# Stores of a FiLM layer: small DMAs for the first rows, whole slabs for the rest

## The chip, the core and the metric

One core of one Trainium2 chip. The metric is the device time of one execution in microseconds; the profile's span (first to last instruction) is about 1.8 us shorter.

## The reference

```python
# x [32, 512, 256], conditioning [32, 64], gamma_proj and beta_proj [64, 256], all float32
gamma = conditioning @ gamma_proj
beta = conditioning @ beta_proj
return x * (1 + gamma[:, None, :]) + beta[:, None, :]
```

16.78 MB are read, 16.78 MB are written, and each element has one multiplication and one addition.

## The kernel before

x lies in SBUF as four slabs of 128 partitions x 32 rows x 256 floats: 32 KB per partition, contiguous in HBM. All four fit at once, so no buffer is reused. Loads are issued by SyncE, the small loads and the stores by ScalarE. Of each group of 16 rows VectorE takes 11 and GpSimd 5; the group is then stored.

```python
LOADS = {0: [8, 24]}          # slab 0 in two loads, the others whole
GROUP = 16
ON_DVE = 11
# ...
nc.scalar.dma_start(out=cond_s, in_=conditioning)
# ... gbproj[:, :dim] <- gamma_proj, gbproj[:, dim:] <- beta_proj, also from nc.scalar
for s in range(SLABS):
    xs = xpool.tile([P, ROWS, dim], f32, name=f"xs{s}")
    # ... nc.sync.dma_start of LOADS.get(s, [ROWS]) rows each
# ... two small matmuls give gamma and beta per slab, in PSUM (gb_p) and in SBUF (gb_s)
for s in range(SLABS):
    # ...
    for r0 in range(0, ROWS, GROUP):
        # ... v = rows r0 to r0+10, w = rows r0+11 to r0+15
        nc.vector.scalar_tensor_tensor(out=v, in0=rows(g_p, nv), scalar=1.0, in1=v,
                                       op0=ALU.add, op1=ALU.mult)
        nc.gpsimd.tensor_tensor(out=w, in0=w, in1=rows(g_s, nw), op=ALU.mult)
        nc.vector.tensor_add(out=v, in0=v, in1=rows(b_p, nv))
        nc.gpsimd.tensor_tensor(out=w, in0=w, in1=rows(b_s, nw), op=ALU.add)
        nc.scalar.dma_start(out=o_v[s, :, r0 : r0 + GROUP, :],
                            in_=xs[:, r0 : r0 + GROUP, :])
```

## Time and profile before

| | before |
|---|---|
| first three runs | 84.46, 86.00, 86.02 us |
| span of the profiled (fast) run | 82.6 us |
| bytes moved, mean rate over the span | 33.69 MB, 408 GB/s |
| VectorE / GpSimd busy | 60% / 56% |
| last addition on VectorE ends | 66.6 us |
| last store packet ends | 81.38 us |

The rows of the page that carry the argument are shown in the prediction: slices, queues, chain, stretches and issues. Two habits help in reading them. The chain of waits ends with the last instruction of a compute engine; where stores follow, look at what the DMA row does after that. And a DMA packet (one contiguous run of bytes that one of the 16 DMA engines moves, here 1 to 32 KB of data) is booked in the slice in which it starts; here most packets last up to 1.2 us, so the GB/s of one slice can be off by a fifth or more in either direction. Where the text speaks of packet records, packets were counted by queue and size in the same trace. A load or store lands when its completion semaphore, the counter that tells the program of it, has its last count; in the first profile of each kernel that is 0.3 to 1.6 us after its last data packet ends.

### The profile page before, as it was taken

Reading aid. Unit: us, or ns where it says so; the run is one execution under the profiler, and the core shown is the slowest. Engines: PE = TensorE matmul, PEld = TensorE weight load, DVE = VectorE, ACT = ScalarE, POOL = GpSimd, SP = SyncE. Lnnn points to the kernel's source line nnn. Section 1 sums busy time; section 2 is a strip of 40 time slices with the busy share of each in tenths; the row PEclk is TensorE's granted clock in tenths of the full one; section 3 lists DMA queues with packets and bytes.
Section 4 is the critical chain, followed back from the end, with each engine's and each line's share of the span. In section 5 each row is a group of like instructions: output and inputs, shape, how many; then the busy total and the mean of one; then the engine's idle time right before and its main releaser. Section 6 shows DMA issues by size and latency. Waiting matters only on the chain.

```text
span 82.6 us, 156 instructions
## 1 busy us (share of the span) xinstructions
PE 9.1 (11%) x10; PEld 2.8 (3%) x10; DVE 49.9 (60%) x18; ACT 3.9 (5%) x9; POOL 46.2 (56%) x22
## 2 busy tenths in 40 slices
PE   0080000899600000000000000000000000000000
PEld 0100000443000000000000000000000000000000
DVE  2011000059999999999999999999999920000000
ACT  0600000034400000000000000000000000000000
POOL 2000000069999999999999999999995000000000
DMA  3899999969969989998889979899999999999992
GB/s 56 337 508 397 389 397 524 460 302 508 508 270 492 508 381 381 413 476 381 381 381 556 460 302 460 381 468 421 429 452 389 468 421 421 460 389 452 437 421 87
DMA packets 2080, 33.69 MB, mean 408 GB/s; under 512 B 288, under 2 KB 416, under 8 KB 416
## 3 DMA queue, kind: packets, MB, share of 16 engines
q1 hardware_dynamic: 720, 16.78, 48.6%
q10 hardware_dynamic: 1360, 16.92, 48.0%
HBM read 16.92 MB, written 16.78 MB: 408 GB/s over the span
## 4 chain that ended last, share of the span: by engine, by line
DVE 49%; DMA 16%; issue 11%; PE 2%; ACTq 1%; ACT 1%
DVE xs L100 30%; DVE xs L103 19%; DMA gbproj<-in_beta_proj_dram 16%; PE gb_p L79 2%; ACTq L50 1%; ACTq L48 0%; ACT gb_s L82 0%; ACT gb_s L85 0%
## 5 line engine op out<-in xcount | busy, mean ns | idle before, releaser
L102 POOL TENSOR_TENSOR xs<-xs,gb_s 128x1280 f32<-128x1280 f32 x8 | 23.0, 2895 | 16.2 <-ACT gb_s L82 16.2
L100 DVE SCALAR_TENSOR_TENSOR xs<-gb_p,xs 128x2816 f32<-128x2816 f32 x8 | 24.7, 3083 | 10.9 <-ACT gb_s L85 10.9
L103 DVE TENSOR_TENSOR xs<-xs,gb_p 128x2816 f32<-128x2816 f32 x8 | 24.7, 3086 | 0.3
L104 POOL TENSOR_TENSOR xs<-xs,gb_s 128x1280 f32<-128x1280 f32 x8 | 23.0, 2893 | 0.0
L79 PE MATMUL gb_p<-gbproj,cond_T 64*128 64x512 f32 x8 | 7.2, 1074 | 8.9 <-DMA gbproj<-in_beta_proj_dram 8.9
L74 DVE COPY cond_T<-cond_T_p 64x512 f32<-64x512 f32 x1 | 0.7, 683 | 4.3 <-PE cond_T_p L72 4.3
L79 PEld LDWEIGHTS gb_p<-gbproj,cond_T 64*128 64x128 f32 x8 | 2.5, 328 | 13.7 <-issue 13.7
L72 PE MATMUL cond_T_p<-rident,cond_s 32*64 32x512 f32 x2 | 1.9, 1065 | 3.9 <-DMA cond_s<-in_conditioning_dram 3.9
L82 ACT ACTIVATE gb_s<-gb_p 128x256 f32<-128x256 f32 x4 | 1.5, 383 | 16.4 <-PE gb_p L79 16.4
L85 ACT COPY gb_s<-gb_p 128x256 f32<-128x256 f32 x4 | 1.5, 367 | 0.0
L82 ACT ACT_TABLE_LOAD x1 | 1.3, 1283 | 2.4 <-issue 2.4
L67 DVE COPY rident<-ident 32x512 f32<-32x512 f32 x1 | 0.4, 416 | 1.2 <-POOL ident masks.py:199 1.2
L72 PEld LDWEIGHTS cond_T_p<-rident,cond_s 32*64 32x64 f32 x2 | 0.3, 202 | 3.9 <-issue 3.9
masks.py:197 POOL MEMSET ident<- 32x32 f32 x1 | 0.1, 114 | 0.3 <-POOLq L121 0.3
masks.py:199 POOL TENSOR_SCALAR_AFFINE_SELECT ident<-ident 32x32 f32<-32x32 f32 x1 | 0.2, 202 | 0.1
L121 POOL MEMSET const-float32-0.0<- 128x1 f32 x1 | 0.1, 103 | 0.2 <-issue 0.2
L121 POOL MEMSET const-bfloat16-1.0<- 128x1 bf16 x1 | 0.1, 106 | 0.0
L121 POOL MEMSET const-uint8-127<- 128x1 uint8 x1 | 0.1, 106 | 0.0
L121 POOL MEMSET const-float32-1.0<- 128x1 f32 x1 | 0.1, 103 | 0.0
## 6 DMA issues: line engine op xcount, KB each, us to landing
out_dram<-xs ACTq DMA_DIRECT2D x8, 2048.0 KB, 18.2
xs<-in_x_dram SPq DMA_DIRECT2D x3, 4096.0 KB, 32.9
xs<-in_x_dram SPq DMA_DIRECT2D x1, 3072.0 KB, 12.2
xs<-in_x_dram SPq DMA_DIRECT2D x1, 1024.0 KB, 4.6
gbproj<-in_gamma_proj_dram ACTq DMA_DIRECT2D x1, 64.0 KB, 9.1
gbproj<-in_beta_proj_dram ACTq DMA_DIRECT2D x1, 64.0 KB, 12.9
cond_s<-in_conditioning_dram ACTq DMA_DIRECT2D x1, 8.0 KB, 3.0
```

Of the source, the lines that this page charges most:

```text
L50: nc.scalar.dma_start(out=gbproj[:, :dim], in_=gamma_proj)
L67: nc.vector.tensor_copy(out=rident.rearrange("p (b g) -> p b g", g=REP), in_=ident.to_broadcast([batch, batch, REP]),)
L72: nc.tensor.matmul(cond_T_p, lhsT=cond_s, rhs=rident, start=True, stop=True)
L74: nc.vector.tensor_copy(out=cond_T, in_=cond_T_p)
L79: nc.tensor.matmul(p_t, lhsT=cond_T[:, s * P : (s + 1) * P], rhs=gbproj, start=True, stop=True)
L82: nc.scalar.activation(out=s_t[:, :dim], in_=p_t[:, :dim], func=mybir.ActivationFunctionType.Identity, bias=1.0, scale=1.0)
L85: nc.scalar.copy(out=s_t[:, dim:], in_=p_t[:, dim:])
L100: nc.vector.scalar_tensor_tensor(out=v, in0=rows(g_p, nv), scalar=1.0, in1=v, op0=ALU.add, op1=ALU.mult)
L102: nc.gpsimd.tensor_tensor(out=w, in0=w, in1=rows(g_s, nw), op=ALU.mult)
L103: nc.vector.tensor_add(out=v, in0=v, in1=rows(b_p, nv))
L104: nc.gpsimd.tensor_tensor(out=w, in0=w, in1=rows(b_s, nw), op=ALU.add)
L121: nc = _bacc.Bacc("TRN2", target_bir_lowering=False, num_devices=1)
```

## The change

The intent, as far as the code shows it: the first store shares the DMA engines with the loads, and small packets there let the loads pass; later stores go out in the longest runs possible, with less fixed cost per packet.

```diff
     LOADS = {0: [8, 24]}
+    STORES = {0: (2, 4, 8, 16, 32), 1: (32,), 2: (32,), 3: (32,)}
 ...
-            nc.scalar.dma_start(out=o_v[s, :, r0 : r0 + GROUP, :],
-                                in_=xs[:, r0 : r0 + GROUP, :])
+            done = r0 + GROUP
+            if done in STORES[s]:
+                e0 = 0
+                for e1 in STORES[s]:
+                    if r0 < e1 <= done or STORES[s] == (ROWS,):
+                        nc.scalar.dma_start(out=o_v[s, :, e0:e1, :], in_=xs[:, e0:e1, :])
+                    e0 = e1
```

The numbers in `STORES` are the rows at which a store ends.

## The prediction

> **What bounds the kernel now.** I read five views of the profile of the kernel before, in this order: the slices with the DMA queues, the chain of waits, the groups with their waits, a table of four stretches, and the list of instructions in order of time. Where they did not suffice I counted the trace's packet records by queue and size.
>
> The slices and the queues come first, because the kernel moves 33.69 MB and does little else:
>
> ```profile
> DMA  3899999969969989998889979899999999999992
> DMA packets 2080, 33.69 MB, mean 408 GB/s; under 512 B 288, under 2 KB 416, under 8 KB 416
> q1 hardware_dynamic: 720, 16.78, 48.6%
> q10 hardware_dynamic: 1360, 16.92, 48.0%
> ```
>
> The reader is to see that the 16 DMA engines are busy from the second slice to the last but one, and that the two queues together take 48.6 + 48.0 = 96.6% of the span of 82.6 us, or 79.8 us. The packet records say the same: the first data packet starts at 1.74 us and the last ends at 81.38, which is 79.64 us; from 4 us on, a count of the packets in flight never falls below about 16. No engine waits for work. (The dips to 6 or 7 in the slices are an effect of booking a packet where it starts; the packets of 32 KB take 1.21 us.) q1 is the loads of x, q10 the stores with the three small loads.
>
> The chain of waits tells another story, and has to be read with care:
>
> ```profile
> DVE 49%; DMA 16%; issue 11%; PE 2%; ACTq 1%; ACT 1%
> ...
> 57.37 3.09 DVE xs L103
> 60.46 3.01 DVE xs L100
> 63.47 0.02 issue
> 63.49 3.09 DVE xs L103
> ```
>
> It ends with the last addition on VectorE, at 66.58 us, 16 us before the span does, because the chain does not follow the stores. What happens in those 16 us is in the stretches (columns: busy time of the engines, clock, DMA share, GB/s) and in the issues:
>
> ```profile
> 2.00:12.50 10.50, 1.93 (x2) 0.29 (x2) 0.68 (x1) 1.28 (x1) 0.00 (x0) 1.00 0.97 400
> 12.50:27.50 15.00, 7.16 (x8) 2.50 (x8) 9.91 (x4) 2.59 (x8) 10.20 (x4) 1.00 1.07 456
> 27.50:50.00 22.50, 0.00 (x0) 0.00 (x0) 22.40 (x8) 0.00 (x0) 22.50 (x9) 1.00 0.97 408
> 50.00:81.00 31.00, 0.00 (x0) 0.00 (x0) 16.48 (x6) 0.00 (x0) 12.97 (x5) 1.00 1.01 431
> ```
> ```profile
> out_dram<-xs ACTq DMA_DIRECT2D x8, 2048.0 KB, 18.2
> xs<-in_x_dram SPq DMA_DIRECT2D x3, 4096.0 KB, 32.9
> ```
>
> Stores alone run at 431 GB/s to the end. A store of 2 MB would take 4.9 us at that rate, yet its median time from issue to landing is 18.2 us: stores stand in a queue. When the last is issued at 66.67 us, 6.27 MB of stores have still to start by the packet records, of which it is 2.10. So the end is set by bytes over DMA rate, and computing is hidden with a reserve of 4.17 MB / 431 GB/s = 9.7 us.
>
> **The skill.** The Trainium skill, "DMA: Bandwidth & Descriptors", section "Where 436 GB/s comes from", gives 435 GB/s as the ceiling of the 16 ports. The trace agrees: 431 with stores alone, and the packet records, spread evenly over their durations, give 433 with loads alone. The same page, "Queues, rings and completion order", says that each engine goes round-robin between the queues that have work, a packet at a time. The trace agrees: from 30 to 48 us one engine's sequence is mostly one load packet of 32 KB, one store packet of 16 KB, in turn. The same page, "Why small descriptors are slow (HBM only)", names a fixed cost per packet. The trace shows it, small: 16 KB take 611 ns and 32 KB 1213 ns, so 602 ns for 16 KB of data and 9 ns fixed; 8 KB (309 ns) and 1 KB (46 ns) fit the same line.
>
> **The change part by part.** The arithmetic on VectorE and GpSimd stays in the same order. Eight stores remain eight stores; only their sizes and moments change.
>
> 1. Packets. Before: 8 stores x 128 partitions = 1024 packets of 16 KB, 64 per engine, 64 x 611 ns = 39.1 us. After, per engine: 16 of 2 KB, 8 of 4 KB, 8 of 8 KB, 8 of 16 KB, 24 of 32 KB, again 64. By the line above, 16 x 84 ns (my estimate) + 8 x 160 (estimate) + 8 x 309 + 8 x 611 + 24 x 1213 = 1.34 + 1.28 + 2.47 + 4.89 + 29.11 = 39.09 us. The long packets save 24 x 9 ns = 0.2 us and the short ones give it back. Sum: zero.
>
> 2. The first rows leave earlier. In the built program the first three stores (rows 0 to 7) wait for VectorE alone, whose part of the group ends at 20.64 + 3.09 = 23.73 us; before, the store of 16 rows waited for GpSimd too and was issued at 25.94. So they are issued at about 23.8, 24.2 and 24.5. The first store took 29.76 - 25.94 = 3.8 us from issue to its first packet, behind load packets already taken up, so I expect the first store packet at about 27.6. On full engines this makes nothing faster; it shifts the order.
>
> 3. Loads get nearly all of the rate while they last. At 27.6 us each engine has 11 load packets of 32 KB to start (5.77 MB / 16 / 32 KB). With one store packet of 2 KB between two loads, they take 11 x 1.225 + 10 x 0.09 = 14.4 us from 28.2 (the packet in hand finishes first), so the last load ends near 42.6 us instead of 48.6. No computing waits for it, before or after: GpSimd takes up slab 3 at 51.5 us and VectorE at 54.25, and their views of waits show no wait for x. Worth zero.
>
> 4. Whole slabs wait for both groups. The first halves of slabs 1 to 3 are issued later by one group (about 4.8 us for slab 1: 42.17 instead of 37.35); the last issue stays at 66.67. The question is whether the stores run dry. From 42.6 us stores run alone with 16.45 MB left. By 54.4 (slab 2 issued) 5.1 MB more are done, 5.4 in all of 8.39 issued: 3.0 MB in hand, 6.9 us. By 66.67, 0.33 + 24.1 us x 431 = 10.7 MB are done of 12.58: 1.9 MB in hand, 4.4 us, against a start of a store of 3.8 us in the worst case seen (cond_s at the start needed 1.4 us from issue to first packet). The reserve shrinks from 9.7 us to 4.4 but is not used up. Cost zero, with the smallest margin of all steps.
>
> 5. Stretched packets. Before, load packets are stretched to 1.35-1.66 us at two moments, about 28.5 and 32.3 us, some 2.5 us after the first two stores were issued: roughly (12 x 0.3 + 8 x 0.22) / 16 = 0.3 us per engine. The change may lose some of this or repeat it. I credit -0.3 us.
>
> End of the wire: 42.6 + 16.45 MB / 431 GB/s (38.2) = 80.8 us, against 81.38. The sum of the parts is -0.3 to -0.6 us, the span 82.6 - 0.4 = 82.2.
>
> **Rivals.** (a) The stores run dry before slab 3 is issued. For it: the margin in 4 is 4.4 us, and it rests on the loads finishing at 42.6. Against: a store issued onto a busy queue need not pay the whole 3.8 us. It would show as a gap of up to 2 us near 70 us, and 86 to 87 us. (b) Loads now finish late because 32 KB store packets take a half share instead of a third, and VectorE waits for slab 3. For it: round-robin by packets. Against: by 42.17 us, when the first store of 32 KB runs is issued, the loads are nearly done, and 16 small packets with two rows of turns stand ahead. It would need the loads to end 9 us later than I work out. It would give 86 to 88 us. (c) Reads and writes mixed cost rate, and less mixing pays: the stretch from 27.5 to 50 us moves 408 GB/s against 431. If all of that were regained, 22.5 x (1 - 408 / 431) = 1.2 us, so 83.2 from the fast mode. Against: spread over their durations the packets of 35 to 50 us move 431 to 433, so most of the difference is booking.
>
> **Range and chances.** The three runs before are 84.46, 86.00 and 86.02 us, and the profiled one 84.35: two modes 1.6 us apart, unexplained by the one profile. The change should give 84.1 in the lower and 85.7 in the upper; not knowing which the median falls in, I say 85.0 us, 83.7 to 86.4. A gain over 2% needs rival (c) together with a fall into the lower mode: 0.08. A loss over 2% needs (a) or (b) in full: 0.05. Within 2%: 0.87.
>
> **What would show it.** Right: DMA slices of 9 to the end as before; the last load lands near 43 us and the small stores stay between 15 and 20 us in the queue; VectorE runs from 17.5 to 66.6 without a wait; the last stores run at 431 GB/s; the span is near 82.2. Step 4 is wrong if a slice near 70 us drops; step 3 if VectorE or GpSimd wait for x; step 1 if 2 KB packets take much more than 84 ns; step 5 if the mixed stretch is much slower or faster. The whole is wrong if the last packet ends before 79 or after 83 us.

## The result

The changed kernel takes 84.50 us (median of 6, 84.39 to 84.61); the kernel before, with three more runs beside it, 84.64 (six runs, two of them at 86.0). Executions over 1.5% slower than the fastest of the same kernel are left out of the means. Ratios here are the mean of one kernel's fast runs over the mean of the other's fast runs of the same rounds, so not quite the ratio of medians: 0.9993, with a 95% interval of 0.9977 to 1.0008. The time is the same. The forecast of 85.0 held as a range and as a class, but against the 86.0 then known it announced 1.0 us less, or 1.2%, and 0.07% came. That forecast of a gain was wrong.

Profile after, slices and queues:

```profile
DMA  3899999899699699996979999998996998999790
DMA packets 2080, 33.69 MB, mean 408 GB/s; under 512 B 288, under 2 KB 416, under 8 KB 800
q1 hardware_dynamic: 720, 16.78, 48.5%
q10 hardware_dynamic: 1360, 16.92, 47.9%
```

The number of packets is the same to the last one, 2080, although 384 more of them are now under 8 KB; the shares of the queues add up to 96.4% of 82.7 us, 79.7 us as before. The issues:

```profile
out_dram<-xs ACTq DMA_DIRECT2D x3, 4096.0 KB, 17.2
out_dram<-xs ACTq DMA_DIRECT2D x1, 2048.0 KB, 22.3
out_dram<-xs ACTq DMA_DIRECT2D x1, 1024.0 KB, 21.5
out_dram<-xs ACTq DMA_DIRECT2D x2, 256.0 KB, 16.9
out_dram<-xs ACTq DMA_DIRECT2D x1, 512.0 KB, 20.3
xs<-in_x_dram SPq DMA_DIRECT2D x3, 4096.0 KB, 23.0
```

A store of 256 KB, 0.6 us of transfer at 431 GB/s, takes 16.9 us to land: it goes one packet of 2 KB at a time between load packets of 32 KB. The loads of whole slabs land in 23.0 us (median) instead of 32.9. (Part of that is only a later issue: the build reuses semaphores differently, so slab 2's load is now issued at 10.73 us instead of 2.10 and slab 3's at 13.97 instead of 10.3. Slab 1's packets fill the queue until 22 us, so it costs nothing. The prediction had not seen it.) The end of the chain:

```profile
57.95 3.09 DVE xs L104
61.04 3.01 DVE xs L101
64.05 0.02 issue
64.07 3.09 DVE xs L104
```

The same last addition, 0.6 us later because gamma and beta landed 0.6 us later in this execution, without a wait in between: no row of the waits of VectorE or GpSimd names x. The stretches of the prediction, after:

```profile
2.00:12.50 10.50, 1.93 (x2) 0.28 (x2) 0.68 (x1) 1.28 (x1) 0.00 (x0) 1.00 1.00 400
12.50:27.50 15.00, 7.16 (x8) 2.50 (x8) 9.35 (x4) 2.59 (x8) 9.63 (x4) 1.00 0.99 422
27.50:50.00 22.50, 0.00 (x0) 0.00 (x0) 22.40 (x8) 0.00 (x0) 22.50 (x9) 1.00 1.01 431
50.00:81.00 31.00, 0.00 (x0) 0.00 (x0) 17.06 (x6) 0.00 (x0) 13.57 (x5) 1.00 1.00 431
```

Here lies a trap. From 27.5 to 50 us the changed kernel moves 431 GB/s against 408, just as rival (c) would have it, and yet ends no sooner: what it gains in the third row it lacks in the second (422 against 456). Cut the same two traces at 27, 44 and 50 us. Before:

```profile
27.00:44.00 17.00, 0.00 (x0) 0.00 (x0) 16.93 (x6) 0.00 (x0) 17.00 (x7) 1.00 1.03 432
44.00:50.00 6.00, 0.00 (x0) 0.00 (x0) 5.96 (x3) 0.00 (x0) 6.00 (x3) 1.00 0.92 393
```

After:

```profile
27.00:44.00 17.00, 0.00 (x0) 0.00 (x0) 16.90 (x7) 0.00 (x0) 17.00 (x7) 1.00 0.97 413
44.00:50.00 6.00, 0.00 (x0) 0.00 (x0) 5.97 (x3) 0.00 (x0) 6.00 (x3) 1.00 1.06 448
```

Now the kernel before is the faster one in the mixed stretch, 432 against 413. The edges decide, since a packet counts where it starts. Spread over their durations, the packets of 27 to 44 us move 421 GB/s before and 431 after, but in the second profile of each kernel 426 and 424, and in the third of the changed one 418: no difference that lasts.

The packet records give the sums. Last load packet: 48.56 us before, 43.54 after. Last store packet: 81.38 before, 81.47 after. Durations of all packets, divided by 16: 79.76 us and 79.70 us.

### The profile page after: what moved, and what is told of

It is laid out like the page before. It is cut to its first block, busy times and chain, and to the rows that moved or that the text cites. A ratio compares the mean times of both kernels' runs of the same rounds, so it can differ in the third digit from the quotient of the medians.

```text
span 82.7 us, 154 instructions
## 1 busy us (share of the span) xinstructions
PE 9.1 (11%) x10; PEld 2.8 (3%) x10; DVE 49.9 (60%) x18; ACT 3.9 (5%) x9; POOL 46.2 (56%) x22
## 2 busy tenths in 40 slices
DMA packets 2080, 33.69 MB, mean 408 GB/s; under 512 B 288, under 2 KB 416, under 8 KB 800
## 4 chain that ended last, share of the span: by engine, by line
DVE 48%; DMA 16%; issue 11%; PE 2%; ACTq 1%; ACT 1%
DVE xs L101 30%; DVE xs L104 19%; DMA gbproj<-in_beta_proj_dram 16%; PE gb_p L80 2%; ACTq L51 1%; ACTq L49 0%; ACT gb_s L83 0%; ACT gb_s L86 0%
## 5 line engine op out<-in xcount | busy, mean ns | idle before, releaser
L83 ACT ACTIVATE gb_s<-gb_p 128x256 f32<-128x256 f32 x4 | 1.5, 384 | 16.9 <-PE gb_p L80 16.9
## 6 DMA issues: line engine op xcount, KB each, us to landing
out_dram<-xs ACTq DMA_DIRECT2D x2, 256.0 KB, 16.9
```

The lines of the kernel that those rows point to most:

```text
L83: nc.scalar.activation(out=s_t[:, :dim], in_=p_t[:, :dim], func=mybir.ActivationFunctionType.Identity, bias=1.0, scale=1.0)
```

## The experiments

Twelve runs were made, three of them of the two kernels unchanged, and all were correct. They ask four things: what the kernels vary by, whether either part alone does something, what a packet costs, and whether anything but the order has changed. The expectations name theories by letters: W, the end is bytes over DMA rate; S and L, a slow start comes by chance or by the change; M, the change keeps the slow state away; T, the program's end has waits of its own; R, whole slabs shrink the reserve of issued stores.

### The kernel before, again

No edit.

> The kernel before, unchanged, a second time: what one kernel varies by. Theory W (the end is bytes over DMA rate, the change only reorders): 84.4 to 84.7 us, last packet again near 81.4. The open points: whether 86.0 us comes back (2 of the first 3 runs of before had it; theory M, that the change removes a slow mode, wants it here in some of the five runs and in none of the changed kernel's), and whether the load packets of 24 KB at the start take 923 ns again as in the first profile of before (theory S, the start varies by chance: anything from 912 to 1010; theory L, the start of the changed kernel is slower by its later issue of slab 2's load: 920 to 930).

Measured: 84.51 us median (84.33 to 84.69, no slow run of 6), ratio 1.0003 (0.9984 to 1.0022). The last packet is again at 81.38 us. The 24 KB packets had a median of 912 ns (mean 944; 937 in the first profile), slab 0 landed at 13.62 us instead of 13.39. So the start varies without any change, and the end doesn't follow.

### The changed kernel, again

No edit.

> The changed kernel, unchanged, a second time. Theory W: 84.4 to 84.6 us, ratio to before 0.998 to 1.001. If the 0.5 us that the changed kernel gained after 27 us (431 against 408 GB/s by the page) is real and its start was slow by chance (theory S), the start may be fast this time and the time 84.0. If theory L holds, the 24 KB packets take 980 to 990 ns again and slab 0 lands at 13.9 us again, 0.5 us later than in before.

Measured: 84.54 us median, one run of 85.59 among six; ratio 1.002 (0.998 to 1.006, wide because that run still counts as fast). This time the start was fast: 24 KB packets 921 ns (median), slab 0 at 13.54 us. Theory L falls, the slow start in the first profile of the changed kernel was chance (a variant of the kernel before, the run on the price of a packet, has such a start too: 986 ns). But 84.0 did not come either: the last load packet is at 43.51 us, in the first profile at 43.54. What the fast start gained was lost at 41 to 42 us, where 12 load packets of 32 KB were stretched, one to 2.0 us. The third profile of the changed kernel (last run below) shows it again, 16 packets at 41.5 us. Per engine, the time of the 24 KB and 32 KB load packets over their shortest duration (912 and 1213 ns) sums as follows:

| run | 24 KB | 32 KB | sum |
|---|---|---|---|
| before | 0.20 us | 0.57 us | 0.77 us |
| before, again | 0.26 | 0.40 | 0.66 |
| after | 0.49 | 0.14 | 0.63 |
| after, again | 0.20 | 0.43 | 0.63 |
| after, third | 0.21 | 0.61 | 0.82 |

The stretching moves (28 to 33 us before, the start or 41 to 42 us after) and its sum does not fall with the change: the largest of the five is the changed kernel's, whose last packet in that profile ends at 81.60 us. Why packets are stretched, these runs do not show.

### The small first stores alone

The edit is against the changed kernel, as in the two runs that follow.

```diff
-    STORES = {0: (2, 4, 8, 16, 32), 1: (32,), 2: (32,), 3: (32,)}
+    STORES = {0: (2, 4, 8, 16, 32), 1: (16, 32), 2: (16, 32), 3: (16, 32)}
```

> Only the first part of the change: rows 0 to 15 of slab 0 in stores of 2, 2, 4 and 8 rows, everything else in halves of 16 rows as before. Packets per engine: 16 of 2 KB, 8 of 4, 8 of 8 and 56 of 16 KB, 88 in all: 16 x 84 + 8 x 159 + 8 x 309 + 56 x 611 ns = 39.3 us against 39.1. Theory W: 84.5 to 84.9 us, the last load landing at 43 to 44 us as in the changed kernel, since the small packets let the loads pass.

Measured: 85.01 us, ratio 1.0062 (1.0046 to 1.0079): slower, by a little, and 0.1 us above what was expected. From its page:

```profile
span 83.2 us, 160 instructions
DMA packets 2512, 33.69 MB, mean 405 GB/s; under 512 B 336, under 2 KB 464, under 8 KB 848
```

432 packets more than before: 384 of data (24 per engine) and 48 that count semaphores for the three more stores. The store packets sum to 39.30 us per engine against 39.11, and the last one is at 81.70 us, 0.3 later. From the last landing (82.06) to the end of the span it is 1.13 us, where before it was 0.83. Together that is 0.6 us in the profile; the timed runs show 0.5. The last load lands at 44.1 us: the small packets do let the loads pass. It earns nothing.

### The whole slabs alone

```diff
-    STORES = {0: (2, 4, 8, 16, 32), 1: (32,), 2: (32,), 3: (32,)}
+    STORES = {0: (16, 32), 1: (32,), 2: (32,), 3: (32,)}
```

> Only the second part: slab 0 in halves of 16 rows as before, slabs 1 to 3 stored whole in runs of 32 KB. Packets per engine 16 of 16 KB and 24 of 32 KB, 40: 9.8 + 29.1 = 38.9 us against 39.1. Theory W: 84.2 to 84.5 us. Slab 0's stores share with the loads as in before, so the last load lands at 48 to 49.5 us, later if 32 KB store packets take half the rate from 43 us on; slab 3's load is wanted at 51.5 us, so nothing waits. If the small packets were needed (the rival): VectorE waits for slab 3 and the time is 86 or more.

Measured: 84.60 us (one slow run of 86.24), ratio 1.0006 (0.9989 to 1.0023), 0.1 us above what was expected. Loads end at 48.76 us, nothing waits for them, and store packets sum to 38.89 us per engine, as worked out. The last packet is nonetheless at 81.45: 0.2 us fewer in the stores, 0.1 us more in the loads (40.23 against 40.10), and 0.17 us more between the last landing and the end.

### All slabs whole

```diff
-    STORES = {0: (2, 4, 8, 16, 32), 1: (32,), 2: (32,), 3: (32,)}
+    STORES = {0: (32,), 1: (32,), 2: (32,), 3: (32,)}
```

> All four slabs stored whole in runs of 32 KB, without the small first stores: four stores, 32 packets of 32 KB per engine, 32 x 1213 ns = 38.8 us against 39.1. The first store is issued at 30 us; from about 33 us load and store packets of 32 KB take turns, so the 7 loads then left per engine take 7 x 2.44 = 17 us and the last load lands near 50.8 us instead of 44.3, 0.8 us before GpSimd wants slab 3. Theory W (bytes over rate, nothing starves): no wait for x, the last store packet at 81.1 to 81.4 us, and the time 84.3 to 84.6, as the last store's semaphore is now the fourth in the final list of waits (theory T below, +0.25 us). Rival (b) of the prediction: GpSimd and VectorE wait for slab 3; if the loads end 1 us later than worked out, still nothing at the end, because the reserve of stores is large.

Measured: 84.59 us (one slow run of 86.33), ratio 1.0006 (0.9989 to 1.0023). A row of its waits, and its packets:

```profile
POOL xs L103 <- DMA xs<-in_x_dram: 1.1, 1, 1.1
...
DMA packets 1504, 33.69 MB, mean 408 GB/s; under 512 B 224, under 2 KB 352, under 8 KB 352
```

With 32 KB packets on both queues the loads are served at half rate and slab 3 lands at 52.55 us, 1.7 us later than I worked out; GpSimd now waits 1.1 us for it. Its last data packet ends at 50.98, near the 50.8 expected; the rest is the small packets that count its semaphore, the last of which starts at 52.18. So rival (b) is real, but it stops there: VectorE takes up slab 3 at 54.3 us as ever, GpSimd catches up, and the last store is issued at 66.70. 576 packets fewer than before bring the last store packet to 81.24 us, 0.14 earlier, and the end of the span takes that back. The small first stores are not needed for the time; they only keep the loads early.

### Slab 2 held back: an experiment that was none

The store of slab 2 was moved behind the computing of slab 3, to let the stores run dry.

```diff
-    STORES = {0: (2, 4, 8, 16, 32), 1: (32,), 2: (32,), 3: (32,)}
+    STORES = {0: (2, 4, 8, 16, 32), 1: (32,), 2: (), 3: (32,)}
 ...
             if done in STORES[s]:
+                if s == 3:
+                    nc.scalar.dma_start(out=o_v[2], in_=slabs[2][:, :, :])
```

> The changed kernel with slab 2 stored only after slab 3 is computed: the reserve of stored work is made to run out, which the changed kernel was 4.4 us away from by the prediction. Slabs 0 and 1 are on HBM at 62.4 us (slab 1 landed at 62.5 in the changed kernel), slabs 2 and 3 are issued near 66.8 and 67.2. Theory W: the DMA engines idle from 62.4 to 66.8 plus the start of a store on an empty queue (1.0 to 1.4 us as at the start of the program), then 16 packets of 1213 ns, 19.5 us: last packet near 87.5, time 90.2 to 91.0, +6 us. If instead the time is set by something other than the DMA engines' work, such as the chain on VectorE, it stays at 84.5. The length of the gap gives what a store on an empty queue costs from issue to first packet.

Measured: 84.44 us, ratio 0.9990 (0.9975 to 1.0004). This does not refute theory W. The issue still waits for slab 2 alone, ScalarE has nothing to do before it, and the trace has it at 54.73 us, where the changed kernel had it. It is the changed kernel once more. The two late starts below replace it.

### The price of a packet

The kernel before, with each slab stored in two DMAs of alternating runs of 2 KB:

```diff
-            nc.scalar.dma_start(out=o_v[s, :, r0 : r0 + GROUP, :],
-                                in_=xs[:, r0 : r0 + GROUP, :])
+            if r0 + GROUP == ROWS:
+                runs = "p (a b c) d -> p b a (c d)"
+                o_r = o_v[s].rearrange(runs, b=2, c=2)
+                x_r = xs[:, :, :].rearrange(runs, b=2, c=2)
+                for b in range(2):
+                    nc.scalar.dma_start(out=o_r[:, b], in_=x_r[:, b])
```

> The kernel before with each slab stored after its second group in two stores of 128 x 8 runs of 2 KB: the same eight stores and bytes, 512 packets of 2 KB per engine in place of 64 of 16 KB. By the line of the prediction (84 ns each): 43.0 us against 39.1, so +3.9 us and 88.4 us, 87.9 to 88.9. If packets of 2 KB overlap and cost only their data (75 ns), 38.4 us and no change; if 2 KB costs more when nothing but such packets runs, over 89.

Measured: 88.01 and 88.12 us, two of four runs slow at 90.0 and 90.1 (hence a median of 89.07). Its page:

```profile
DMA  2999999997999979979899999999999999999992
DMA packets 9248, 33.69 MB, mean 390 GB/s; under 512 B 288, under 2 KB 416, under 8 KB 8608
```

7168 packets more on full engines cost 3.6 us against the 84.5 us of before: 7168 / 16 x 8 ns. The forecast was 3.9. The packets have a median of 84 ns and a mean of 87. Their records overlap a little: the stores' sum grows by 5.3 us per engine, but the last packet ends only 3.7 us later (85.10). So the line of the prediction (data plus 9 ns) holds for the single record, the price on the clock is about 8 ns, and it says why the change could not gain by its packets: it has as many as before.

### Small loads in halves: semaphores at the end, and a late start

The edit is against the kernel before.

```diff
-    nc.scalar.dma_start(out=cond_s, in_=conditioning)
+    nc.scalar.dma_start(out=cond_s[:16], in_=conditioning[:16])
+    nc.scalar.dma_start(out=cond_s[16:], in_=conditioning[16:])
 # ... gamma_proj and beta_proj likewise, 32 partitions at a time
```

> The kernel before with the three small loads each in two halves by partitions: the same packets and bytes, 19 DMAs in place of 16. Theory T (the tail): SyncE waits at the end for one completion semaphore after the other, about 62 ns each, in a fixed order; with 16 DMAs the last store has the last semaphore of the list, with 19 the first, so five more waits follow the last landing: +0.31 us, time 84.8, ratio 1.003 to 1.004, as the page of the run with small stores only showed (last landing 82.06, span 83.20, against 81.74 and 82.57). If that run was slower because of its packets alone, this kernel is at 84.5.

Measured: 84.61 us (one slow run of 86.92), ratio 1.0006 (0.9990 to 1.0022), not the 1.003 expected. In the one profile theory T is to be seen: SyncE's waits after the last landing at 81.73 us come at 81.75, 81.81, 81.88, 81.94, 82.00 and 82.06 us, and the span is 82.87; before there is one, at 81.76, and 82.57. In the timed runs that 0.3 us does not stand out (spans of the fast runs 82.7 to 83.0 against 82.6 to 82.9), so what it is worth there stays open.

By accident this run showed something more useful. The halves of beta landed late, and VectorE started 5 us late; a row of its waits, and the DMA slices:

```profile
DVE xs L103 <- ACT gb_s L88: 12.5, 1, 12.5
...
DMA  2899999989979979999999999999999999999990
```

VectorE runs from 22.8 us instead of 17.5, the last store is issued at 71.97 us instead of 66.67, and the last packet ends at 81.39. Computing is not what the kernel waits for, by more than 5 us.

### The same late start for the changed kernel

The edit of the last run, in the changed kernel.

> The changed kernel with the small loads in halves as in the run on lanes, which by accident started VectorE 5.3 us later (22.8 against 17.5) and issued the kernel before's last store at 71.97 without any loss. Theory R (the whole slabs shrink the reserve of stores in hand from 9.7 us to 4.4): here the last store is issued near 72.0, and the engines are done with slab 2 at 71.9 (it landed at 72.16 in the changed kernel), so they idle for the time that a store on an empty queue needs from issue to its first packet: 1.0 to 1.4 us by the loads at the start, up to 3.8 by the first store. Last packet 82.7 to 83.2, time 85.6 to 86.2 (ratio 1.013 to 1.02). If the changed kernel has as much reserve as before: 84.6.

Measured: 85.63 us, ratio 1.0143 (1.0129 to 1.0157). Here the same delay costs 1.2 us against the kernel before. Of it the last packet accounts for 0.95 us (82.42 against 81.47; 82.7 to 83.2 was expected), and in the profile the rest is again the waits after the last landing (1.14 us against 0.83), which the run before this one had too. The stretches:

```profile
60.00:71.00 11.00, 0.00 (x0) 0.00 (x0) 10.93 (x4) 0.00 (x0) 8.04 (x3) 1.00 0.99 429
71.00:74.00 3.00, 0.00 (x0) 0.00 (x0) 0.65 (x1) 0.00 (x0) 0.00 (x0) 1.00 0.82 350
```

Slab 2's packets end at 71.3 to 71.8 us, the last store is issued at 71.72 and its first packets start at 72.57. A store on an empty queue needs 0.85 us from issue to first packet (0.84 and 0.85 in the two idle moments of the next run); with the time that each engine had already waited for the issue, the 16 engines stand still for 1.07 us on average. Theory R is borne out by a case in which it had to lose time.

### A later start still, for both

Gamma and beta are loaded from the queue of x, behind slab 1 (the same edit in both kernels):

```diff
-    nc.scalar.dma_start(out=gbproj[:, :dim], in_=gamma_proj)
-    nc.scalar.dma_start(out=gbproj[:, dim:], in_=beta_proj)
 # ... in the loop over slabs, after the loads of slab s:
+        if s == 1:
+            nc.sync.dma_start(out=gbproj[:, :dim], in_=gamma_proj)
+            nc.sync.dma_start(out=gbproj[:, dim:], in_=beta_proj)
```

For the changed kernel:

> The changed kernel with gamma and beta loaded on the queue of x behind slab 1, so that computing starts near 25.5 us, 8 us late; the last store is issued near 74.7. Theory R: the engines idle from about 72 to 74.7 plus 1.0 to 1.4 us, and the last slab takes 9.7 us more: last packet 85.4 to 85.9, time 88.3 to 89. The build also takes the first two slabs in alternation, which may cost an idle moment near 47 to 50 us that the later gap swallows. If the end is bytes over rate whatever the order: 84.5.

For the kernel before:

> The kernel before with the same late gamma and beta. Theory R: stores of 16 rows keep the queue filled, the engines are done with the last but one near 76.5 us and the last is issued near 74.8, so that its start is just hidden: last packet near 81.5 to 82, time 84.5 to 85.2. With the run before, this gives what the whole slabs give up: 3.5 to 4.5 us between two kernels of equal time when computing is early. If the late start costs both alike: 88.

Measured: 88.68 us, ratio 1.0508 (1.0493 to 1.0522), for the changed kernel, and 84.46 us, ratio 1.0018 (0.9999 to 1.0037), for the kernel before, just under the 84.5 expected. Stretches of the changed kernel, then of the kernel before:

```profile
50.00:64.00 14.00, 0.00 (x0) 0.00 (x0) 14.00 (x6) 0.00 (x0) 14.00 (x6) 1.00 0.84 363
64.00:67.00 3.00, 0.00 (x0) 0.00 (x0) 3.00 (x2) 0.00 (x0) 3.00 (x2) 1.00 0.40 175
```
```profile
50.00:64.00 14.00, 0.00 (x0) 0.00 (x0) 14.00 (x6) 0.00 (x0) 14.00 (x6) 1.00 1.01 431
64.00:67.00 3.00, 0.00 (x0) 0.00 (x0) 3.00 (x2) 0.00 (x0) 3.00 (x2) 1.00 1.02 437
```

Both have VectorE and GpSimd busy in every microsecond of these stretches, and in both VectorE starts at 26.1 to 26.2 us, 8.6 us later than in the kernel before; only the stores differ. The kernel before keeps the engines full. The changed one leaves them idle for 4.2 us, the sum of the gaps by the packet records, and its last packet ends 4.3 us later than in the changed kernel (85.74 against 81.47). The size was right, the place was not: I expected the gap near 72 to 76 us, and it came near 52 to 54 and 64 to 66, because the build takes slabs 0 and 1 in alternation, and stores of whole slabs then wait twice.

### The slow state

No edit: the changed kernel a third time.

> The changed kernel once more, for the slow state alone: so far before and the variants without small first stores were slow (over 85.8 us) in 11 of 56 runs, the changed kernel and the variants with small first stores in none over 85.8 and one of 85.59 in 22. Theory M (the change keeps the slow state away): none of 6 over 85.8 here, and one to four of the runs of before beside it. If the state does not depend on the kernel: one or two here. Six runs cannot settle it; all runs will be pooled.

Measured: 84.36 to 84.72 us in four runs, 85.72 and 86.02 in two; ratio 1.0017 (1.0002 to 1.0032). Theory M falls. Pooled, before had 8 of 45 runs over 85.5 us (2 of 6, 1 of 11, 0 of 6, 3 of 11, 2 of 11), the changed kernel 3 of 18. The state comes with the execution; that this change alters its share, these counts do not show. Its time lies within the span (84.5 instead of 82.7 us, granted clock 1.0 in both); no profile of it was kept, so its cause stays open.

No experiment points to a version that beats both kernels. The fewest packets (all slabs whole) moved the last one by 0.14 us, and the timed runs show no gain from it.

## Why the prediction was right or wrong

- **The bound** was right. All kernels here move the same bytes; those whose engines never stood still ended their last packet between 81.24 and 81.70 us, except the one with 7168 more packets; delays of computing by 5 and 8.6 us did not move the end of the kernel before.
- **The reserve** of the kernel before was read with a small slip: at 66.67 us the packet records have 6.11 MB of stores still to start, not 6.27. The 9.7 us stands, as packets already started belong to it (see step 4).
- **Step 1** was right: 39.09 us of store packets per engine forecast, 39.09 measured, 39.11 before. The estimates of 84 and 160 ns measured 84 and 159.
- **Step 2** was right within the variation of the start: first stores at 24.33, 24.73 and 25.22 us in the first profile and 23.91, 24.31 and 24.80 in the second; first store packet at 27.74 and 27.31 us (27.6 forecast).
- **Step 3** was right in its mechanism and its worth of zero, and 0.6 us off in the size: the engines' last load packets ended at 43.2 us on average, not 42.6.
- **Step 4** was right. When the last store was issued at 67.24 us the engines had 4.1 to 4.5 us of stores in hand (slab 2's packets end at 71.33 to 71.79); 4.4 was forecast. Before it is 9.5 to 9.9 (66.67 to 76.20-76.52), against 9.7. Rival (a) did not come about here and did in both late starts; its price of a start was 0.85 us, not up to 3.8, which is the price behind load packets.
- **Step 5** failed: "I credit -0.3 us". The stretched load packets turn up at another place; their sum fell by 0.14 us between the first two profiles and by 0.03 between the second two, and in the third of the changed kernel it is above both of before. And the **end of the wire** compared an average over engines (80.8 us) with the last packet of before (81.38); the average of before is 81.20, and of after 81.21. That mismatch is 0.2 of the 0.6 us; the other 0.4 is step 3's end of the loads, 0.6 us too early, less 0.2 us because the stores after it took 38.0 us and not 38.2. The -0.3 to -0.6 us were made of these, and nothing of them was measured.
- **Range and chances** failed in their centre: "not knowing which the median falls in, I say 85.0 us". The middle of two modes is a time that hardly any execution has, and set against a median of three that had fallen into the upper mode it announced a gain of 1.2% which the working did not contain. The working said 0.3 us or 0.4%, the same for both modes (84.1 and 85.7). The runs had the lower mode in four of five executions of either kernel, so fast against fast was the comparison to make: 84.4 and no change. The class, 0.87 for within 2%, was right; the range held because it spanned both modes.
- **Rival (c)** was turned down for the right reason, and the redrawn stretches show it.

## What to carry to other kernels

As long as the DMA engines were never idle, the order and grouping of stores moved no time in these runs beyond what the count of packets explains (8 to 9 ns each on its engine), except perhaps the 0.3 us of waits at the end. Grouping stores more coarsely still has a price that the time hides: it spends the reserve of work in hand, here from 9.7 to 4.4 us, and a change that delayed computing by 5 us then cost 1.4% in the one kernel and nothing in the other. Distrust a difference in GB/s that changes its sign when the window's edges are moved.

## What the Trainium skill lacked or had wrong

- "DMA: Bandwidth & Descriptors", section "Where 436 GB/s comes from", says that for transfers between HBM and SBUF the HBM side (about 358 GB/s per core) binds. Here one core moves 431 to 433 GB/s in steady loads and in stores, near the page's other ceiling of 435. The sentence lacks its condition, which stands elsewhere on the page: 358 is the share with both cores of a pair streaming. What the neighbouring core did here is not known.
- The same page, section "Latency and other measured facts", gives about 0.6 us to the first byte of such a DMA. Here it was 0.85 us for a store on an empty queue and 3.4 to 4.4 us, over all profiles, for the first store behind load packets of 32 KB; the page has no figure for a queue that shares its engines.
- The same page, section "Measured (HBM→SBUF, 128 partitions, SWDGE, issued from GpSimd)", has a rule to batch DMAs to 1 MiB or more, drawn from DMAs that GpSimd issued. It does not say what a small DMA costs behind other work. In the changed kernel, whose ScalarE issued them, stores of 256 KB cost only their packets, 84 ns for each 2 KB.
- No page has the time of SyncE's waits at the end of a program: one completion semaphore after the other, 62 ns each, in a fixed order, so that the span depends on which of them the last store has (one wait after the last landing or six, 0.3 us, in the profiles; not resolved in the timed runs).
